# A relative-bias table stored with the head as its inner index, built first and loaded on the weights' queue

## The chip, the cores and the metric

The kernel runs on one core of a Trainium2 chip. The metric is the device time of one execution in microseconds (us), lower is better. Engines are named as in the profile: PE is TensorE's matmul, PEld its weight load, DVE VectorE, ACT ScalarE, POOL GpSimd, SP SyncE. DMAs are issued by two engines here: SP (queue q1, which carries the weights) and ACT (queue q10).

## What is computed

One decoder layer on 256 tokens of width 1024, in float32: softmax attention with 8 heads and a relative-position bias, then a mixture of 32 experts of which each token uses 4. Each sublayer is followed by a layer norm of the scaled residual sum. The attention, cut to what matters (there is one block of 256 keys, so every query sees all keys at or before it):

```python
qkv = (x @ w_in).reshape(B, S, 3, H, Dh)
s_own = einsum('bhqd,bhjd->bhqj', q, k) * Dh ** -0.5 + rel_t[:, t5_bucket(rel_own)]
s_own = where(rel_own >= 0, s_own, -inf)
o = einsum('bhqj,bhjd->bhqd', softmax(s_own), v)
return o @ w_out
```

Here `rel_own` is the distance from query to key, `t5_bucket` maps it to one of 32 buckets, and `rel_t` is the transpose of the learnt table `rel_bias` (32 buckets by 8 heads). The expert weights are nearly all of the 424 MB that are read.

## The kernel before

**Buffers.** SBUF holds 13 slots of 2 MB (`slot`, L102). Three are taken for good: `xhl`, `BT_xT` (the bias table BT in its first half, the transposed input xT in its second) and `QT_KTt`. The others hold weight tiles and their split copies `whl`. `todo` lists the weight tiles in the order of their use: six tiles of `w_in` in the order 0, 2, 1, 3, 4, 5, two of `w_out`, then for every expert four `w_gu` and two `w_dn`. `fetch` (L127) issues the next tile on SP, in pieces; `prefetch` (L140) does so whenever a slot is free. So the weights run ahead of the work by as many slots as are free, and no further.

**Order.** The order on each engine is the order of the program (`manual_schedule`). Each DMA takes one of eight completion semaphores in turn (DMAHW0 to DMAHW7, SP's and ACT's DMAs together), and a DMA waits until the one that had its semaphore before it has landed.

**The projections.** A loop over n = 0 to 11 (L394) takes half a tile of `w_in` per turn. A weight half tile is split into a high and a low part (`split`, L156: cast on ACT, L176; difference on DVE, L165), one turn ahead. In turns 0 to 7 `proj_qk` (L299) makes 48 matmuls of 256 columns per turn (L310 to L312), for Q and K; in turns 8 to 11 `proj_v` makes 24 of 512 columns. After two turns `evac` (L315) copies four PSUM banks out, on DVE and ACT. The banks of turns 4 and 5 are used again in turns 6 and 7.

**The attention between them.** After turn 4 `scores` (L348) makes the scores of head 0, after turn 5 of head 1, and so on. One turn later `softmax` (L354) scales them and adds the bias (`scalar_tensor_tensor` on DVE, L359, the only reader of BT), takes the maximum (L362) and the exponential (ACT, L364). Heads follow up to turn 11.

**The bias.** `rb` (32 by 8) and a one-hot `oh` (32 by 256) are loaded on SP behind the first weight tile (L248, L249). In turn 1 `rel_bias` (L261) multiplies them to 8 by 256 and copies that behind 127 columns of -1e30 into `rrow` (8 by 383, head as row). In turn 2 ACT stores it to DRAM as `rd`, in turn 3 ACT loads BT from it (L272): partition p, head h takes 256 numbers from column p on, so 1,024 runs of 1 KB with 1 MB in all. L359 reads BT backwards.

**The start.** Nine warm-up matmuls (L256) run on PE while xT and the first weight tile w0 arrive, w0 in six pieces (L245, then `load` at L247 for the last two).

The first lines of the softmax before, which the change touches:

```python
for t, (lo, hi) in enumerate(SPANS):
    nc.vector.scalar_tensor_tensor(p[:, lo:hi], ps[:, lo:hi], SC, BT[:, hh, :hi - lo][:, ::-1],
                                   op0=OP.mult, op1=OP.add)
```

Of the kernel before, what the change touches and what calls it, by code (L numbers as in the profile page):

```python
# [11 lines left out]
F32 = mybir.dt.float32  # L12
# [10 lines left out]
S, D, H, DH = 256, 1024, 8, 128  # L23
# [8 lines left out]
NEG = -1.0e30  # L32
# [28 lines left out]
def tile_decoder_layer(ctx: ExitStack, tc, a, out):  # L61
    nc = tc.nc
# [3 lines left out]
    dr = ctx.enter_context(tc.tile_pool(name="dr", bufs=1, space=DRAM))  # L66
    pm = ctx.enter_context(tc.tile_pool(name="pm", bufs=1, space=PSUM))

    def bank(name):
        return pm.tile([128, 512], F32, name=name)  # L70
# [11 lines left out]
    def small(name, w, p=128, dt=F32):  # L82
        return cst.tile([p, w], dt, name=name)

    c = small("c", C_W)
# [16 lines left out]
    def slot(name, dt=F32):  # L102
        used[0] += 1
        assert used[0] <= W_SLOTS
        return wp.tile([128, SLOT], dt, name=name, tag="w")
# [8 lines left out]
    def source(key):  # L114
        kind, e, k = key
        if kind == "in":
            return a["w_in"][e]
        return a["w_out"][k] if kind == "out" else a["w_gu" if kind == "gu" else "w_dn"][e, k]
# [8 lines left out]
    def fetch(pieces=1):  # L127
        key = todo.pop()
        src = source(key)
        t = slot("w").rearrange("p (k c) -> p k c", k=src.shape[1])  # L130
        load(t, src, pieces)
        w_tiles[key] = t

    def load(t, src, pieces):
        k = src.shape[1]
        for i in range(pieces):
            ks = slice(i * k // pieces, (i + 1) * k // pieces)
            nc.sync.dma_start(t[:, ks], src[:, ks])

    def prefetch():  # L140
        while todo and W_SLOTS - used[0] > reserve[0]:
            fetch(1 if len(todo) > 1 else 4)
# [74 lines left out]
    hp = hctx.enter_context(tc.tile_pool(name="hp", bufs=1))  # L217
# [5 lines left out]
    g7, sg = KTt[:, :512], KTt[:, 512:1024]  # L223
    aT = g7.rearrange("p (j s c) -> p j s c", j=4, s=2)
    Y = KTt[:, 1024:].rearrange("p (b c) -> p b c", b=2)
    BT, QT, KTt = (t.rearrange("p (h s) -> p h s", h=H) for t in (BT, QT, KTt))
    rb = hp.tile([32, H], F32, name="rb")
    oh_wg = hp.tile([128, 256], F32, name="oh_wg")
    oh, wg = oh_wg[:32], oh_wg.rearrange("p (k e) -> p k e", k=KT)
    rrow = hp.tile([H, 383], F32, name="rrow")  # L230
    zeros = hp.tile([128, 128], BF, name="zeros")
    zeros4 = zeros[:, None, :].to_broadcast([128, 4, 128])
    p3 = pp.tile([128, 3, 384], F32, name="p3", tag="p3")
    router = hp.tile([128, KT + 1, NE], F32, name="router")
    wr, br = router[:, :KT], router[:, KT]
    oh_, ol_ = xh, xl

    xT3 = xT.rearrange("p (k s) -> p k s", k=KT)
    key0 = todo.pop()
    w0 = w_tiles[key0] = slot("w").rearrange("p (k c) -> p k c", k=KT)  # L240
# [4 lines left out]
        nc.sync.dma_start(w0[:, i:i + 1], source(key0)[:, i:i + 1])  # L245
    nc.sync.dma_start(xT3[:, X_PARTS[2]], a["xT"][:, X_PARTS[2]])
    load(w0[:, 4:], source(key0)[:, 4:], 2)  # L247
    nc.sync.dma_start(rb, a["rel_bias"])  # L248
    nc.sync.dma_start(oh, a["onehot"])  # L249
    for _ in range(2):  # L250
        fetch(2)
    nc.vector.memset(ones, 1.0)
    nc.vector.memset(eps, EPS)
    warm = bank("tp2")
    for i in range(9):
        nc.tensor.matmul(warm[:, :128], ones, ones, start=i == 0, stop=i == 8)  # L256
    nc.vector.memset(rrow[:, 0:127], NEG)
    nc.vector.memset(zeros, 0.0)
    rd = dr.tile([H, 383], F32, name="rd")

    def rel_bias():  # L261
        pr = bank("tp2")
        nc.tensor.matmul(pr[:H, :256], rb, oh, start=True, stop=True)
        nc.vector.tensor_copy(rrow[:, 127:383], pr[:H, :256])
        nc.sync.dma_start(c, a["consts"])
        nc.sync.dma_start(router.rearrange("p k e -> p (k e)"), a["router"])

    def rel_bias_out():
        nc.scalar.dma_start(rd, rrow)

    def rel_bias_in():
        nc.scalar.dma_start(BT, bass.AP(tensor=rd.tensor, offset=rd.offset, ap=[[1, 128], [383, H], [1, S]]))  # L272

    def split_x(s):
        xhf, xlf = (t.rearrange("p k s -> p (k s)") for t in (xh, xl))
# [12 lines left out]
    def split_next(key):  # L288
        n = ahead.get(key)
        if n and n not in split_done:  # L290
            split_done.add(n)
            split(n, act_copy)
# [22 lines left out]
    def evac(blk, dst):  # L315
        ps = open_ps[blk]
        if blk < 4:
            h0 = (blk % 2) * 4
            for j in range(4):
                (nc.scalar.copy if j % 2 else nc.vector.tensor_copy)(dst[:, h0 + j, :], ps[j][:, :S])  # L320
        else:
            c0 = (blk % 2) * 512
            nc.scalar.copy(V[:, 0, c0:c0 + 512], ps[0])
            nc.vector.tensor_copy(V[:, 1, c0:c0 + 512], ps[1])
# [17 lines left out]
    SC = DH ** -0.5  # L342
# [5 lines left out]
    def scores(hh):  # L348
        ps = bank(next(rows_bank))
        nc.tensor.matmul(ps[:, 0:128], QT[:, hh, 0:128], KTt[:, hh, 0:128], start=True, stop=True)  # L350
        nc.tensor.matmul(ps[:, 128:384], QT[:, hh, 128:256], KTt[:, hh, :], start=True, stop=True)
        P[hh] = ps

    def softmax(hh):  # L354
        ps = P[hh]
        p = p3[:, hh % 3]
        st = hp.tile([128, 8], F32, name="sst", bufs=3)
        for t, (lo, hi) in enumerate(SPANS):
            nc.vector.scalar_tensor_tensor(p[:, lo:hi], ps[:, lo:hi], SC, BT[:, hh, :hi - lo][:, ::-1],  # L359
                                           op0=OP.mult, op1=OP.add)  # L360
        for t, (lo, hi) in enumerate(SPANS):
            nc.vector.tensor_reduce(st[:, t:t + 1], p[:, lo:hi], axis=AX.X, op=OP.max, negate=True)  # L362
        for t, (lo, hi) in enumerate(SPANS):
            nc.scalar.activation(p[:, lo:hi], p[:, lo:hi], AF.Exp, bias=st[:, t:t + 1],  # L364
                                 accum_out=st[:, 2 + t:3 + t])
        P[hh] = p, st

    def softmax_norm(hh):
        p, st = P[hh]
        nc.vector.reciprocal(st[:, 4:6], st[:, 2:4])  # L370
        for t, (lo, hi) in enumerate(SPANS):
            nc.vector.tensor_scalar(p[:, lo:hi], p[:, lo:hi], st[:, 4 + t:5 + t], None, op0=OP.mult)


    def p_transpose(hh):
        p, st = P.pop(hh)
        ps = bank(next(one_bank))
        for i in range(3):
            s = slice(i * 128, (i + 1) * 128)
            nc.tensor.transpose(ps[:, s], p[:, s], ident)  # L380
        nc.scalar.copy(QT[:, hh, :], ps[:, :256])
        nc.scalar.copy(KTt[:, hh, :128], ps[:, 256:384])
# [11 lines left out]
    for n in range(12):  # L394
        blk, i = ORDER[n // 2], n % 2
        last = n == 11
        if not last:
            split_next(("in", blk, i))
        if n == 1:
            rel_bias()  # L400
            reserve[0] = 1
            prefetch()
        if n == 2:
            rel_bias_out()
        if n == 3:
            rel_bias_in()
        for hh in score_at.get(n - 1, []):
            softmax(hh)
        if last:
            for hh in score_at.get(n - 1, []):  # L410
                softmax_norm(hh)
            split_next(("in", blk, i))
        (proj_qk if blk < 4 else proj_v)(blk, i)
        if i == 1:
            evac(blk, QT if blk < 2 else KTt)
        if not last:
            for hh in score_at.get(n - 1, []):
                softmax_norm(hh)
        for hh in score_at.get(n, []):
            scores(hh)  # L420
        for hh in trans_at.get(n, []):
            p_transpose(hh)
# [219 lines left out]
    h = x  # L642
# [219 lines left out]
    for p in range(NE // 2):  # L862
        ahead_pair = p + 1 < NE // 2
        for s in range(2):
            e = 2 * p + s
# [83 lines left out]
    lo, hi = HALVES  # L949
# [53 lines left out]
```

## Time and profile before

| | |
|---|---|
| median of 3 runs | 1087.15 us (1087.0 to 1087.31) |
| the profiled execution's own time | 1087.11 us |
| its span, first to last instruction | 1085.3 us |
| PE busy | 975.1 us (90% of the span) |
| DVE, ACT busy | 265.6 us (24%), 180.5 us (17%) |
| read from HBM | 423.91 MB, 392 GB/s over the span |
| first matmul of the projections / end of the last one | 5.42 us / 109.6 us |

What lies around the span is 1.8 us. The profile is one execution, taken by the hardware profiler. A busy PE there is not a PE at its peak, since matmuls overlap in the records. The idle time of an engine is put down to what ended it. The profile cuts the span in 40 slices of 27.1 us; one digit is the share of a slice in tenths.

### The profile page before, as it was taken

To read this page: it belongs to the slowest core of one execution; us is meant where nothing else is said; L and a number is where in the kernel's file an instruction comes from. 1 tells how busy PE (TensorE), PEld (TensorE's weight loads), DVE (VectorE), ACT (ScalarE), POOL (GpSimd) and SP (SyncE) were. 2 spreads that over 40 slices of the span, in tenths; PEclk is the share of its full clock that TensorE was granted. 3 is DMA by queue.
4 is the path that set the end of the run, shared out by engine and by line. 5 is a ranking of instruction groups with operands and counts; after the bars stand their busy time and mean duration, and the time that the engine had idled before them with its cause. 6 is when DMAs were issued, how large, how long until landed. Compare 5 with 4: busy or idle time off the path is not lost. (4 is left out here: it accounts for less than half of the span.)

```text
span 1085.3 us, 11473 instructions
## 1 busy us (share of the span) xinstructions
PE 975.1 (90%) x4886; PEld 450.4 (41%) x4886; DVE 265.6 (24%) x555; ACT 180.5 (17%) x345; POOL 15.7 (1%) x10
## 2 busy tenths in 40 slices
PE   9649989999999999888989889999989898988893
PEld 8648764334343443232424243343423243333331
DVE  5237562121222211112121232212111212121104
ACT  5126431101011110010101010011101010101112
POOL 0000030000000000000000000000000000000001
PEclk9869989999999999999999989999999999999997
DMA  9964579999999999999999999999999999999981
GB/s 358 422 243 152 161 297 406 428 427 428 428 426 428 428 425 430 427 427 429 426 429 428 413 423 426 428 428 427 427 428 427 428 429 428 428 428 426 429 372 40
DMA packets 33204, 425.74 MB, mean 392 GB/s; under 512 B 3672, under 2 KB 5120, under 8 KB 7456
## 3 DMA queue, kind: packets, MB, share of 16 engines
q1 hardware_dynamic: 31824, 422.87, 92.8%
q10 hardware_dynamic: 1328, 2.11, 0.6%
q8 instruction: 40, 0.66, 0.2%
q14 instruction: 12, 0.10, 0.0%
HBM read 423.91 MB, written 1.06 MB: 392 GB/s over the span
## 5 line engine op out<-in xcount | busy, mean ns | idle before, releaser
L677 PE MATMUL hg<-w,QT_KTt 128*64 128x512 f32 x960 | 250.8, 599 | 54.5 <-DMA w<-in_w_gu 54.2
L677 PE MATMUL hu<-w,QT_KTt 128*64 128x512 f32 x960 | 248.6, 594 | 0.0
L705 PE MATMUL yp<-w,QT_KTt 128*64 128x512 f32 x1008 | 226.8, 595 | 1.3 <-ACT QT_KTt L695 1.3
L684 DVE TENSOR_SCALAR QT_KTt<-hg 128x512 f32<-128x512 f32 x32 | 22.1, 692 | 665.5 <-PE hg L677 665.5
L677 PEld LDWEIGHTS hg<-w,QT_KTt 128*64 128x64 f32 x960 | 66.0, 137 | 194.9 <-issue 127.0
L705 PEld LDWEIGHTS yp<-w,QT_KTt 128*64 128x64 f32 x1008 | 70.6, 137 | 142.3 <-issue 127.9
L677 PEld LDWEIGHTS hu<-w,QT_KTt 128*64 128x64 f32 x960 | 71.2, 137 | 135.7 <-issue 135.7
L685 ACT ACTIVATE QT_KTt<-QT_KTt 128x512 f32<-128x512 f32 x32 | 20.1, 629 | 477.7 <-DVE QT_KTt L684 477.7
L709 ACT COPY QT_KTt<-yp 64x512 f32<-64x512 f32 x63 | 36.5, 580 | 233.4 <-PE yp L705 225.9
L663 PEld LDWEIGHTS tp<-OH,BT_xT 128*128 128x128 f32 x480 | 58.4, 199 | 12.0 <-issue 11.2
L663 PE MATMUL tp<-OH,BT_xT 128*128 128x128 f32 x480 | 62.7, 286 | 0.0
L165 DVE TENSOR_TENSOR whl<-w,whl 128x1024 fp32r<-128x1024 f32 (+1 forms) x36 | 41.2, 1187 | 29.4 <-ACT whl L176 29.4
L310 PE MATMUL o<-xhl,whl 128*128 128x256 f32 x48 | 15.0, 312 | 25.1 <-DVE QT_KTt L320 24.5
L176 ACT CAST whl<-w 128x1024 fp32r<-128x1024 f32 (+1 forms) x36 | 32.7, 954 | 11.3 <-DMA w<-in_w_in 4.7
L569 DVE TENSOR_SCALAR QT_KTt<-tp,c 128x128 f32<-128x128 f32 x60 | 20.5, 405 | 44.1 <-PE tp L663 44.1
L733 PE MATMUL tp<-QT_KTt 128*128 128x512 f32 x60 | 30.7, 593 | 0.0
L733 PE MATMUL o<-QT_KTt 128*128 128x512 f32 x60 | 29.8, 618 | 0.0
L571 ACT ACTIVATE QT_KTt<-tp,c 128x128 f32<-128x128 f32 x60 | 22.6, 457 | 36.3 <-PE tp L663 36.3
L695 ACT COPY QT_KTt<-tp 128x512 f32<-128x512 f32 x32 | 19.2, 600 | 42.9 <-PE tp L694 35.9
L686 DVE TENSOR_SCALAR hu<-hu 128x512 f32<-128x512 f32 x32 | 22.4, 700 | 3.1 <-PE hu L677 0.2
L694 PE MATMUL tp<-c,QT_KTt 128*128 128x128 f32 x128 | 20.0, 280 | 3.4 <-DVE QT_KTt L688 3.2
L688 DVE SCALAR_TENSOR_TENSOR QT_KTt<-hu,QT_KTt 128x512 f32<-128x512 f32 x32 | 22.1, 691 | 1.1
(258 smaller groups left out, 758.7 us busy)
## 6 DMA issues: line engine op xcount, KB each, us to landing
w<-in_w_gu SPq DMA_DIRECT2D x128, 2048.0 KB, 39.1
w<-in_w_dn SPq DMA_DIRECT2D x63, 2048.0 KB, 39.1
w<-in_w_in SPq DMA_DIRECT2D x3, 2048.0 KB, 21.1
w<-in_w_in SPq DMA_DIRECT2D x4, 1024.0 KB, 11.1
w<-in_w_out SPq DMA_DIRECT2D x2, 2048.0 KB, 28.3
w<-in_w_dn SPq DMA_DIRECT2D x4, 512.0 KB, 31.8
w<-in_w_in SPq DMA_DIRECT2D x4, 256.0 KB, 5.7
w<-in_w_in SPq DMA_DIRECT2D x2, 512.0 KB, 8.5
```

The lines of the kernel that those rows point to most:

```text
L165: nc.vector.tensor_tensor(lo[:, s], w[:, s], hi[:, s].bitcast(F32), op=OP.subtract)
L176: nc.scalar.copy(o, i)
L569: nc.vector.tensor_scalar(o, i, g, b, op0=OP.mult, op1=OP.add)
L571: nc.scalar.activation(o, i, AF.Identity, scale=g, bias=b)
L663: nc.tensor.matmul(ps[:, k * 128:(k + 1) * 128], h[:, t, kk * 128:(kk + 1) * 128], OH[:, t].rearrange("p s c -> p (s c)"), start=t == 0, s ...
L677: nc.tensor.matmul(hgu[i][s * 64:(s + 1) * 64], xg(k), w[:, kk, q * 512:(q + 1) * 512], start=False, stop=k == KT - 1)
L684: nc.vector.tensor_scalar(g7, hgu[0], LIMIT, None, op0=OP.min)
L686: nc.vector.tensor_scalar(u7, u7, LIMIT, -LIMIT, op0=OP.min, op1=OP.max)
L688: nc.vector.scalar_tensor_tensor(sg, u7, 1.0, g7, op0=OP.add, op1=OP.mult)
L705: nc.tensor.matmul(y_ps[s], aT[:, kk % 4, kk // 4, :], w[:, k, HALVES[s ^ swap]], start=kk == 0, stop=kk == KT - 1)
L709: copy(Y[s * 64:(s + 1) * 64, s ^ swap, :], y_ps[s])
L733: nc.tensor.matmul(po, GT[:, cb, t, :], Y[:, cb, :], start=True, stop=True)
```

## The change

`rel_bias` and `rel_bias_out`, `rel_bias_in` of turns 1 to 3 are gone. In their place, ahead of the loop: ACT issues the loads of `rb` and `oh` before anything else. PE multiplies them after the warm-up, with 128 distances as output rows and 8 heads as columns, twice. DVE copies the result into `rrow` (now 128 by 3 by 8). ACT stores it to `rd` (now 383 rows of 8 heads) in two DMAs: 127 rows of -1e30, and 256 rows of bias. SP then loads BT between the second and the third tile of `w_in`: partition p takes 2,048 consecutive numbers from row p on. L359 reads BT with a step of 8 numbers, backwards. The loads of `consts` and `router` stay in turn 1.

```diff
-    BT, QT, KTt = (t.rearrange("p (h s) -> p h s", h=H) for t in (BT, QT, KTt))
+    BT_rows, BT = BT, BT.rearrange("p (s h) -> p s h", h=H)
+    QT, KTt = (t.rearrange("p (h s) -> p h s", h=H) for t in (QT, KTt))
...
-    rrow = hp.tile([H, 383], F32, name="rrow")
+    rrow = hp.tile([128, 3, H], F32, name="rrow")
...
+    nc.scalar.dma_start(rb, a["rel_bias"])
+    nc.scalar.dma_start(oh, a["onehot"])
...
-    nc.sync.dma_start(rb, a["rel_bias"])
-    nc.sync.dma_start(oh, a["onehot"])
-    for _ in range(2):
-        fetch(2)
...
+    rd = dr.tile([383, H], F32, name="rd")
+
+    def rel_rows(row, ap):
+        return bass.AP(tensor=rd.tensor, offset=rd.offset + row * H, ap=ap)
+
+    pr = bank("yp")
+    for i in range(2):
+        nc.tensor.matmul(pr[:, i * H:(i + 1) * H], oh[:, i * 128:(i + 1) * 128], rb, start=True, stop=True)
+    nc.vector.tensor_copy(rrow[:, :2], pr[:, :2 * H].rearrange("p (i h) -> p i h", i=2))
+    nc.scalar.dma_start(rel_rows(0, [[H, 127], [1, H]]), rrow[:127, 2])
+    nc.scalar.dma_start(rel_rows(127, [[H, 128], [128 * H, 2], [1, H]]), rrow[:, :2])
+    fetch(2)
+    nc.sync.dma_start(BT_rows, rel_rows(0, [[H, 128], [1, S * H]]))
+    fetch(2)
...
-            nc.vector.scalar_tensor_tensor(p[:, lo:hi], ps[:, lo:hi], SC, BT[:, hh, :hi - lo][:, ::-1],
+            nc.vector.scalar_tensor_tensor(p[:, lo:hi], ps[:, lo:hi], SC, BT[:, :hi - lo, hh][:, ::-1],
```

How this moves the instructions is seen at two places. The first is the head of ACT's order, before (L numbers of the kernel before):

```order
L176 ACT_TABLE_LOAD
L176 CAST xhl<-BT_xT 128x256 [waits DMAHW0_49]
L176 CAST whl<-w 128x512 [waits DMAHW1_49]
L176 CAST xhl<-BT_xT 128x256 [waits DMAHW2_49]
L176 CAST whl<-w 128x512 [waits DMAHW3_49]
```

and with the change (L numbers of the changed kernel):

```order
L239 DMA rb<-in_rel_bias 32x8
L240 DMA oh_wg<-in_onehot 32x256
L267 DMA rd<-rrow 127x8 [waits DVE_49]
L268 DMA rd<-rrow 128x2x8 [waits DMAHW1_49,DVE_49]
L176 ACT_TABLE_LOAD
L176 CAST xhl<-BT_xT 128x256
L176 CAST whl<-w 128x512 [waits DMAHW3_49]
```

Four DMAs stand ahead of ACT's table load and its first casts; the fourth waits for DVE's copy into `rrow`. The second place is SP's queue from the third input part of xT on, before:

```order
L246 DMA BT_xT<-in_xT 128x1024
L138 DMA w<-in_w_in 128x1024
L138 DMA w<-in_w_in 128x1024 [waits DMAHW0_49]
L248 DMA rb<-in_rel_bias 32x8 [waits DMAHW1_49]
L249 DMA oh_wg<-in_onehot 32x256 [waits DMAHW2_49]
L138 DMA w<-in_w_in 128x2048 [waits DMAHW3_49]
L138 DMA w<-in_w_in 128x2048 [waits DMAHW4_49]
L138 DMA w<-in_w_in 128x2048 [waits DMAHW5_49]
L138 DMA w<-in_w_in 128x2048 [waits DMAHW6_49]
```

and with the change:

```order
L249 DMA BT_xT<-in_xT 128x1024 [waits DMAHW2_49]
L138 DMA w<-in_w_in 128x1024 [waits DMAHW3_49]
L138 DMA w<-in_w_in 128x1024 [waits DMAHW4_49]
L138 DMA w<-in_w_in 128x2048 [waits DMAHW5_49]
L138 DMA w<-in_w_in 128x2048 [waits DMAHW6_49]
L270 DMA BT_xT<-rd 128x2048 [waits DMAHW7_49,DMAHW1_49]
L138 DMA w<-in_w_in 128x2048 [waits DMAHW0_49]
L138 DMA w<-in_w_in 128x2048
```

`rb` and `oh` are gone from SP, BT stands among the tiles of `w_in`, and the semaphores that SP waits on are others. Of these, DMAHW4 was last used by the first store of `rd` (127 rows), DMAHW1 by the second: the sixth piece of w0 (the second row of 128x1024) waits until the first store has landed, and BT waits for the second.

## Rows read from the trace of the kernel before

**Rows 1.** The page's 40 slices: DMA share in tenths, rate.
```profile
DMA  9964579999999999999999999999999999999981
GB/s 358 422 243 152 161 297 406 428 427 428 428 426 428 428 425 430 427 427 429 426 429 428 413 423 426 428 428 427 427 428 427 428 429 428 428 428 426 429 372 40
```
**Rows 2.** Waits of PE, whole span: us in total, times, longest us.
```profile
PE hg L677 <- DMA w<-in_w_gu: 54.2, 48, 2.3
PE o L310 <- DVE QT_KTt L320: 24.5, 1, 24.5
```
**Rows 3.** Waits of DVE, 0 to 200 us.
```profile
DVE p L359 <- DMA BT_xT<-rd: 28.5, 1, 28.5
```
**Rows 4.** DMA issues: line's tile, engine, count, KB each, median us to landing.
```profile
BT_xT<-rd ACTq DMA_DIRECT2D x1, 1024.0 KB, 37.1
...
BT_xT<-in_xT SPq DMA_DIRECT2D x1, 128.0 KB, 2.6
```
**Rows 5.** Windows by stage: PE, PEld, DVE, ACT, POOL busy; PEclk, DMA share, GB/s.
```profile
50.00:60.00 10.00, 0.00 (x0) 0.00 (x0) 0.00 (x0) 0.00 (x0) 0.00 (x0) 0.50 1.01 421
60.00:70.00 10.00, 1.14 (x5) 1.17 (x6) 2.52 (x9) 1.91 (x7) 0.00 (x0) 0.50 0.49 200
...
80.00:90.00 10.00, 10.00 (x61) 8.88 (x60) 7.29 (x19) 4.94 (x14) 0.00 (x0) 1.00 0.14 34
...
160.00:170.00 10.00, 10.00 (x48) 3.30 (x46) 2.93 (x17) 2.84 (x4) 0.00 (x0) 1.00 0.67 247
170.00:180.00 10.00, 9.87 (x64) 5.78 (x62) 4.04 (x8) 2.61 (x6) 0.00 (x0) 1.00 1.01 434
```
**Rows 6.** Timeline of PE around its long wait: start us, us, instruction.
```profile
43.77 0.60 PE L351 MATMUL hu<-QT_KTt 128*128 128x256 f32 x2
68.86 0.55 PE L310 MATMUL o<-xhl,whl 128*128 128x256 f32 x1 [24.49 <-DVE QT_KTt L320]
...
71.56 0.37 PE L310 MATMUL o<-xhl,whl 128*128 128x256 f32 x1
...
72.00 0.28 PE L310 MATMUL o<-xhl,whl 128*128 128x256 f32 x1
72.12 0.28 PE L311 MATMUL o<-xhl,whl 128*128 128x256 f32 x1
```
**Rows 7.** Timeline of all engines at the start.
```profile
0.74 1.28 ACT L176 ACT_TABLE_LOAD   x1 [0.74 <-PEq L995]
...
1.06 4.21 PE L256 MATMUL tp<-ones 128*128 128x128 f32 x18 [1.06 <-DVE ones L252]
...
3.32 0.40 ACT L176 CAST xhl<-BT_xT 128x256 fp32r<-128x256 f32 x1 [1.30 <-DMA BT_xT<-in_xT]
...
4.75 0.62 ACT L176 CAST whl<-w 128x512 fp32r<-128x512 f32 x1 [1.02 <-DMA w<-in_w_in]
...
13.03 1.14 ACT L176 CAST whl<-w 128x512 fp32r<-128x512 f32 x2 [0.21 <-DMA w<-in_w_in]
...
13.49 0.59 PE L263 MATMUL tp<-oh_wg,rb 32*8 32x256 f32 x2
```
**Rows 8.** Timeline of ACT, 14 to 31 us.
```profile
20.06 0.37 ACT L320 COPY QT_KTt<-tp 128x256 f32<-128x256 f32 x1 [0.35 <-PE tp L312]
...
24.78 0.55 ACTq L269 DMA_DIRECT2D rd<-rrow  x1
...
30.00 0.39 ACTq L272 DMA_DIRECT2D BT_xT<-rd  x1
```
**Rows 9.** Groups of DVE by form, 60 to 130 us.
```profile
L362 DVE TENSOR_REDUCE sst<-p 128x1 f32<-128x256 f32 x8 | 3.3, 411 | 0.0
...
L359 DVE SCALAR_TENSOR_TENSOR p<-hu,BT_xT 128x256 f32<-128x256 f32 x4 | 1.7, 416 | 0.0
...
L489 DVE TENSOR_REDUCE BT_xT<-oh_wg 128x32 f32<-128x256 f32 x1 | 0.6, 625 | 0.0
```
**Rows 10.** Timeline of PE at the end of the projections.
```profile
110.61 0.70 PE L387 MATMUL tp<-QT_KTt,BT_xT 128*128 128x256 f32 x2 [0.30 <-ACT QT_KTt L382]
```

More of the change, by code (lines that the diff above doesn't have):

```diff
@@ L256, in tile_decoder_layer @@
         nc.tensor.matmul(warm[:, :128], ones, ones, start=i == 0, stop=i == 8)
-    nc.vector.memset(rrow[:, 0:127], NEG)
+    nc.vector.memset(rrow[:, 2], NEG)
     nc.vector.memset(zeros, 0.0)
[L259 to L272, printed above, removed]
+    rd = dr.tile([383, H], F32, name="rd")
[10 more added lines that the diff above has]
+    fetch(2)
     def split_x(s):
@@ L399, in tile_decoder_layer @@
         if n == 1:
-            rel_bias()
+            nc.sync.dma_start(c, a["consts"])
+            nc.sync.dma_start(router.rearrange("p k e -> p (k e)"), a["router"])
             reserve[0] = 1
             prefetch()
[L403 to L406, printed above, removed]
         for hh in score_at.get(n - 1, []):
```

## The prediction, made before the changed kernel was run

> **What bounds the kernel now.** I read the slices first [rows 1]. From about 165 us to the end the DMA rate stands at 428 GB/s with its engines 9 tenths busy or more. There the weights' stream sets the pace, and PE waits for it, 54.2 us in 48 pieces [rows 2]. The expert phase can't be shortened by anything in this change, but it can begin earlier. For the DMA is not full before it: the third to the sixth slice (54 to 163 us) run at 243, 152, 161 and 297 GB/s. There the missing rate is (185 + 276 + 267 + 131) / 428 x 27.1 us = 54 us of an idle stream. It idles because the 13 slots are full and the work that frees them is late. The stream becomes full for good at about 165 us [rows 5]. So the end is that moment plus fixed bytes: a microsecond gained in the work ahead of 165 us is a microsecond at the end, as long as no more than those 54 us are taken.
>
> What is late in that work? PE's second long wait is one of 24.5 us, for a DVE copy at L320 [rows 2]. DVE had itself waited 28.5 us for the load of BT [rows 3]. The timeline of PE has the place: scores of head 1 at 43.77 us, next projection matmul at 68.86 [rows 6]. The copies that free the PSUM banks of turns 4 and 5 stand behind `softmax(0)` on DVE, and that waits for BT. BT was issued at 30.0 us [rows 8] and took 37.1 us to land [rows 4], with DMA full until about 65 us [rows 5].
>
> Why 37.1 us for 1 MB: its 1,024 runs are 64 for each of 16 DMA engines, 0.58 us each. A weight row of 16 KB takes 16,384 B x 16 / 427 GB/s = 0.61 us. So a run of BT had about one weight row beside it each time.
>
> **The change, part by part.** The sum is made against the profiled execution: 1087.11 us, of which 1085.3 are span. The median of the three runs is 1087.15, so no correction is needed.
>
> *The wait goes: -24.5 us.* SP now issues BT behind the second tile of `w_in`. Its 128 rows of 8 KB stand in the line of the weights and cost 1 MB / 425 GB/s = 2.5 us. If both stores to `rd` have landed by 15 us, BT lands near 20 us. Turn 5's softmax wants it at about 39 us (67.2 us less the 28.5 waited [rows 3]). The work that comes then takes the place of the wait: after the scores at 43.77 us PE goes straight on, since the bank it needs has its last matmul about 1 us before the turn's end and the copy takes 0.4 us. What is late next is nothing on PE up to the end of the projections. The tile of turn 6 is the fourth; 10 MB in all, BT counted, have landed by 28 us at 425 GB/s.
>
> *The slow clock after it: -1.3 us.* During the wait the granted clock fell to 0.5 [rows 5]. Twelve matmuls then ran at half rate, 68.86 to 71.56 us [rows 6], 2.7 us where twelve take 1.44 at the pitch of 0.12 that follows. Without the wait there is no fall.
>
> *The start is later: +1.7 us.* This is the change's new cost. ACT issues four DMAs ahead of its table load, and the fourth waits for DVE's copy, that for two PE matmuls, and those stand behind the warm-up, which ends at 1.06 + 4.21 = 5.3 us [rows 7]. Loads of `rb` and `oh`, issued at about 0.8 and 1.2 us, land before that (2.6 us for a piece of xT [rows 4]). The two matmuls take at most the 0.59 us of the old one with 256 columns [rows 7], the copy and the semaphores some 0.3 (a copy of 256 columns takes 0.37 on ACT [rows 8]), the store's issue 0.4 to 0.55 [rows 8]. The table load of 1.28 us, off the path before [rows 7], begins near 6.6 and ends at 7.9. The first two casts (0.40 and 0.62 [rows 7]) follow, and PE's first projection matmul starts near 8.9 us instead of 5.4. Most of these 3.5 us are made good: before, turns 0 and 1 waited for pieces of w0 (the casts of the last one at 13.03 us waited for a DMA [rows 7]) and ended at 20.0 us (ACT's last copy waits for PE until 20.06 [rows 8]). Now PE has 96 matmuls of 0.12 us, 11.5 us, which end at 20.4; with twelve at half rate, as after the long wait, 21.7. Against 20.0 that is +1.7. The least is +0.4, with a clock that stays up; the most depends on the sixth piece of w0, below.
>
> *The strided read: +0.6 us.* L359 now steps 32 bytes in BT. No such read of L359 is in the trace; the nearest is L489, a reduction that steps through 256 elements, 625 ns against 411 for the unit-step one of L362 [rows 9]. That is 0.84 ns an element, 0.32 us for a head's 384, 2.6 us for eight on DVE. PE covers it in turns 5 to 10, where DVE is busy 7.29 of 10 us and PE all of it [rows 5]. At the end of the projections the cover is gone: PE waits 0.30 us there already [rows 10]. So I take the last two heads, 0.6 us; the bounds are 0 and 2.6. The Trainium skill ("SBUF — State Buffer", the note on cachelines under the DMA port swizzle) speaks against this layout: SBUF has 16-byte lines, each crossing to a new line pays a penalty, and 4 float32 is as far as one can step free. It gives no size; by it every element pays, and L489, at 625 ns, agrees that there is a price. If it were double what L489 shows, the sum would be 0.6 us higher.
>
> *Edits at nothing.* The old `rel_bias` work in turns 1 to 3 (a matmul of 0.59 us, two issues) goes from under other waits. The bytes of BT stay 1 MB. The stores are 12 KB.
>
> Sum: -24.5 - 1.3 + 1.7 + 0.6 = -23.5, so 1087.1 - 23.5 = **1063.6 us**.
>
> **The rivals.** *Slower: the first store holds the weights' queue.* SP's sixth piece of w0 waits for the 127-row store. If these rows, a number that 16 doesn't divide, all go through one DMA engine and each is served like a run of BT, they take 127 x 0.58 = 74 us and land at 75. The piece lands 2.6 us after its issue, is cast in 0.6, and leaves PE two slices of 1.44; so turn 1 ends 6.1 us after the store. Landing at 15.6 us costs nothing beyond the 21.7 above, each microsecond later costs one, and break-even is at 39 us. At 75 the time is 1063.6 + 59 = 1123 us. The Trainium skill ("DMA: Bandwidth & Descriptors", on why a DMA increments its semaphore by 16) says that a DMA from ACT uses the largest count up to 16 that divides the outer sizes, so 127 partitions use one engine. No row here shows it. For the rival: the old store was never timed on landing. Against: the 0.58 us are a weight row's own time, and while SP waits, only 8 DMAs with 8 rows per engine stand ahead, done by 10 us; what is left of the 127 then runs alone.
>
> *A part given back:* the store lands between 20 and 39 us; 1068 to 1087.
>
> *Bytes decide:* the stream is the bound throughout and nothing comes earlier; 1087 us. Against it stand the 54 idle us.
>
> *The change doesn't do what it says:* BT is still late or another wait takes over in turns 5 to 6; half the gain, 1075 us. For it: BT waits for the second store, which stands behind the first. Against: some 20 us of slack.
>
> **Chances.** The forecast 0.83, a part given back 0.06, slower 0.04, bytes 0.03, BT still late 0.04. The range: the bounds of the forecast are -25.8 + 0.4 = 1061.7 and, with 2.6 for the read and the store at 20 us (+4.4), 1070.0; I take 1061.0 to 1069.5, which leaves out the other cases and little more. A measurement tells 0.2% (2.2 us) from no change. Faster by more than that: 0.83 + 0.06 + 0.04 = 0.93; within it 0.03; slower 0.04.
>
> **What would show it.** In the changed kernel's profile: no wait of DVE L358 for BT, PE without a gap at 44 to 69 us and no clock of 0.5 there; first projection matmul near 8.9 us, turn 1 ending near 21.7; L358 near 630 ns for 256 columns; DMA full for good near 142 us; PE's waits for `w_gu` still near 54 us. Wrong: a first store that lands after 16 us, a DMA gap in the first 30 us that PE feels, or a new wait of PE before 110 us.

## The result and the profile after

| | before | after |
|---|---|---|
| median | 1087.23 us (4 runs, 1087.0 to 1089.35) | **1064.06 us** (4 runs, 1063.89 to 1064.37) |
| the profiled execution: time, span | 1087.11, 1085.3 us | 1064.1, 1062.2 us |
| ratio | | 0.9782, 95% interval 0.9769 to 0.9795 |

The forecast was 1063.6 us, in a range of 1061.0 to 1069.5. L numbers below are those of the kernel named: in the changed one the projections are L309 to L311, their copies L319, the softmax's first step L358.

The waits of PE over the whole span (us in total, times, longest us) are the first view:

```profile
PE hg L673 <- DMA w<-in_w_gu: 55.8, 50, 2.2
...
PE o L309 <- ACT whl L176: 3.0, 1, 3.0
```

The 24.5 us of [rows 2] are gone. The waits for the weights are 55.8 us against 54.2: the expert phase is what it was, only earlier. New is one wait of 3.0 us, at the start. The timeline of DVE where the 28.5 us wait for BT stood [rows 3] (start us, us, instruction, idle time before it):

```profile
43.80 0.93 DVE L358 SCALAR_TENSOR_TENSOR p<-hg,BT_xT 128x128 f32<-128x128 f32 x2
44.65 0.61 DVE L361 TENSOR_REDUCE sst<-p 128x1 f32<-128x128 f32 x2
45.77 0.42 DVE L319 COPY QT_KTt<-o 128x256 f32<-128x256 f32 x1 [0.51 <-PE o L311]
```

No idle time stands ahead of L358, and the copy that frees a bank for turn 6 follows at 45.77 us. It waits for PE, not PE for it. The windows (PE, PEld, DVE, ACT, POOL busy; PEclk, DMA share, GB/s):

```profile
50.00:60.00 10.00, 10.00 (x84) 9.90 (x84) 6.89 (x16) 4.23 (x12) 0.00 (x0) 1.00 1.02 428
60.00:70.00 10.00, 10.00 (x52) 8.42 (x51) 5.70 (x14) 6.04 (x16) 0.00 (x0) 1.00 1.01 428
140.00:145.00 5.00, 5.00 (x26) 1.69 (x24) 1.46 (x6) 0.82 (x1) 0.00 (x0) 1.00 0.89 301
145.00:150.00 5.00, 5.00 (x25) 1.52 (x21) 0.69 (x1) 0.03 (x1) 0.00 (x0) 1.00 1.01 433
```

PE is busy throughout 50 to 70 us at the full clock, where [rows 5] had 1.14 us of work at 0.50. The DMA engines are full for good from 140 to 145 us on, not from 160 to 170. The page's slices show the same: the stretch without full DMA has become shorter by about one slice.

```profile
DMA  9986689999999999999999999999999999999981
GB/s 355 426 344 221 251 362 428 429 428 427 428 426 429 427 429 426 427 428 428 429 428 426 415 426 429 427 429 426 428 428 426 429 426 428 426 430 426 430 364 41
```

The DMA issues (KB, us to landing) and the waits of SP's queue from 0 to 40 us tell how BT came in time. The first store of `rd` held the queue for 0.7 us, BT waited 7.3 us for the second one, was issued at 15.3 us and landed 6.1 us later, at 21.4, where turn 5 wants it at 43.8. So it had 22 us to spare.

```profile
BT_xT<-rd SPq DMA_DIRECT2D x1, 1024.0 KB, 6.1
...
rd<-rrow ACTq DMA_DIRECT2D x1, 8.0 KB, 9.6
```

```profile
SPq L270 <- DMA rd<-rrow: 7.3, 1, 7.3
...
SPq L138 <- DMA rd<-rrow: 0.7, 1, 0.7
```

The start is where something was lost. Its timeline:

```profile
4.58 2.72 SPq L138 DMA_DIRECT2D w<-in_w_in  x4
4.87 0.52 PEld L265 LDWEIGHTS yp<-rb,oh_wg 32*128 32x128 f32 x4
4.87 0.61 PE L265 MATMUL yp<-rb,oh_wg 32*128 32x8 f32 x4
5.51 0.17 DVE L266 COPY rrow<-yp 128x16 f32<-128x16 f32 x1 [4.41 <-PE yp L265]
5.72 0.43 ACTq L268 DMA_DIRECT2D rd<-rrow  x1
6.18 1.28 ACT L176 ACT_TABLE_LOAD   x1 [6.18 <-DVE rrow L266]
...
8.45 0.58 PE L309 MATMUL o<-xhl,whl 128*128 128x256 f32 x1 [2.97 <-ACT whl L176]
```

The chain is as forecast: matmul, copy, store, table load, cast. The first projection matmul starts at 8.45 us, before it was 5.42. But the windows of the same stretch show a clock of 0.50 (1.2 GHz) for longer than the working allowed:

```profile
7.00:8.00 1.00, 0.00 (x0) 0.00 (x0) 0.09 (x1) 0.99 (x3) 0.00 (x0) 0.93 1.11 397
8.00:9.00 1.00, 0.55 (x2) 0.50 (x2) 0.91 (x2) 1.00 (x3) 0.00 (x0) 0.50 0.98 363
...
13.00:14.00 1.00, 1.00 (x6) 1.00 (x6) 1.00 (x3) 0.95 (x2) 0.00 (x0) 0.50 0.98 410
14.00:15.00 1.00, 1.00 (x8) 1.00 (x7) 1.00 (x3) 0.00 (x0) 0.00 (x0) 0.66 1.06 443
15.00:16.00 1.00, 1.00 (x10) 1.00 (x9) 0.41 (x1) 0.51 (x1) 0.00 (x0) 1.00 1.04 442
```

PE idled from 5.48 to 8.45 us; the clock fell in that time and came back between 14 and 15 us. 27 matmuls, from 8.45 to 14.67 us, ran at half rate. Turn 1 ended with this copy on ACT, 3.1 us later than the 20.06 of [rows 8]:

```profile
23.16 0.37 ACT L319 COPY QT_KTt<-tp 128x256 f32<-128x256 f32 x1 [0.35 <-PE tp L311]
```

What stands under the projections' end, at last:

```profile
87.71 0.70 PE L386 MATMUL tp<-QT_KTt,BT_xT 128*128 128x256 f32 x2 [0.30 <-ACT QT_KTt L381]
```

This row answers to [rows 10]. It comes 110.61 - 87.71 = 22.9 us earlier, and the span is 23.1 us shorter: what was gained ahead of it arrived at the end.

### The profile page after: what moved, and what is told of

Same layout as the page of the kernel before. It is cut to its first block, busy times and chain, and to the rows that moved or that the text cites. A ratio compares the mean times of both kernels' runs of the same rounds, so it can differ in the third digit from the quotient of the medians.

```text
span 1062.2 us, 11476 instructions
## 1 busy us (share of the span) xinstructions
PE 973.1 (92%) x4888; PEld 449.7 (42%) x4888; DVE 267.6 (25%) x555; ACT 179.9 (17%) x345; POOL 15.7 (1%) x10
## 5 line engine op out<-in xcount | busy, mean ns | idle before, releaser
L673 PE MATMUL hg<-w,QT_KTt 128*64 128x512 f32 x960 | 250.9, 599 | 55.9 <-DMA w<-in_w_gu 55.8
L659 PE MATMUL tp<-OH,BT_xT 128*128 128x128 f32 x480 | 61.7, 283 | 0.0
L165 DVE TENSOR_TENSOR whl<-w,whl 128x1024 fp32r<-128x1024 f32 (+1 forms) x36 | 41.2, 1187 | 24.9 <-ACT whl L176 24.8
L683 DVE TENSOR_TENSOR QT_KTt<-QT_KTt 128x512 f32<-128x512 f32 x32 | 21.9, 684 | 0.0
## 6 DMA issues: line engine op xcount, KB each, us to landing
w<-in_w_in SPq DMA_DIRECT2D x3, 2048.0 KB, 20.3
```

What stands on the lines that cost most here:

```text
L165: nc.vector.tensor_tensor(lo[:, s], w[:, s], hi[:, s].bitcast(F32), op=OP.subtract)
L659: nc.tensor.matmul(ps[:, k * 128:(k + 1) * 128], h[:, t, kk * 128:(kk + 1) * 128], OH[:, t].rearrange("p s c -> p (s c)"), start=t == 0, s ...
L673: nc.tensor.matmul(hgu[i][s * 64:(s + 1) * 64], xg(k), w[:, kk, q * 512:(q + 1) * 512], start=False, stop=k == KT - 1)
L683: nc.vector.tensor_tensor(g7, g7, sg, op=OP.mult)
```

## The experiments

Three things changed at once: how BT lies (8 KB rows, read by L358 with a step), when it is made (ahead of all, not in turns 1 to 3), and on which queue it is loaded. Theory A, that of the prediction: only the time of landing counts, against 44 us. The rivals: it is the large rows, or the queue. Early alone, layout alone and queue alone were each run; layout and queue together but late were not. The start was a question of its own. All the ratios are to runs of the kernel before on the same chip, whose medians were 1088.04 and 1088.43 us there. One row is followed through all of the experiments: the first matmul of the p-transposes after the projections, 110.61 us before and 87.71 after.

**Early, but in the old layout** (two kernels, against the changed one). BT goes back to 1,024 runs of 1 KB and L358 to unit step; ACT issues the load behind its first casts in the one, SP behind the second tile of `w_in` in the other.

```diff
-    rd = dr.tile([383, H], F32, name="rd")
+    rd = dr.tile([H, 383], F32, name="rd")
...
-        nc.tensor.matmul(pr[:, i * H:(i + 1) * H], oh[:, i * 128:(i + 1) * 128], rb, start=True, stop=True)
+    nc.tensor.matmul(pr[:H, :256], rb, oh, start=True, stop=True)
...
+    nc.scalar.dma_start(rd, rrow)
+    def rel_bias_in(engine):
+        engine.dma_start(BT, bass.AP(tensor=rd.tensor, offset=rd.offset, ap=[[1, 128], [383, H], [1, S]]))
...
+    rel_bias_in(nc.scalar)
```

The other has `rel_bias_in(nc.sync)` between the two fetches.

On ACT's queue:

> Early alone: the table is made as early as in the changed kernel, but with the head as outer index (1,024 runs of 1 KB, unit-step reads), and ACT issues its load at about 14 us, on its own queue. Theory A (each run is served beside one weight row, so 64 runs an engine set the landing): 16 runs beside 8 KB rows of 0.3 us, some beside the short rows of the constants, the rest beside 16 KB rows of 0.61 us: 26 to 34 us from issue to landing, so at 40 to 48 us, at or just behind turn 5's demand at 43.8; PE waits 0 to 6 us, total 1063.5 to 1069 us. Theory B (the load was late only because it was issued late, the layout is of no account): it lands about 6 to 10 us after its issue, no wait, 1064.0 us or less.

On SP's queue:

> Early and on the weights' queue, but with the head as outer index: 1,024 runs of 1 KB between the second and the third tile, unit-step reads. Theory A (in the line of the weights a run has nothing beside it, so the queue matters and not the run): landing within 4 to 8 us of the issue, L358's two forms back at 284 and 416 ns, total 1064.0 within 0.7 us, with the same late start. Theory B (short runs are slow by themselves): landing 20 us or more after the issue with the weight tiles behind it late; the tile of turn 4 would come after 25 us and PE would wait, 1066 us or more. If the strided read costs what I took for it (0.6 us), this kernel is that much faster than the changed one; if PE hides all of it, the same.

Measured: 1064.42 us (1064.12 to 1065.05), ratio 0.9782 [0.9765, 0.9798], and 1064.35 us (1064.02 to 1064.96), ratio 0.9781 [0.9765, 0.9798]. Both agree with the changed kernel's 0.9782. The DMA issue and the softmax of the one on ACT's queue:

```profile
BT_xT<-rd ACTq DMA_DIRECT2D x1, 1024.0 KB, 30.6
```

```profile
43.50 0.62 DVE L355 SCALAR_TENSOR_TENSOR p<-hg,BT_xT 128x128 f32<-128x128 f32 x2
```

Issued at 12.77 us, BT landed at 43.4, as long after its issue as Theory A had it (26 to 34 us), and was read at 43.50, with no wait. It was just in time, and any later landing would have been a wait. SP's weight loads stood 14.7 us in this kernel for the landing of BT, since a semaphore is taken in turn; that cost nothing in the total. The issue of the one on SP's queue:

```profile
BT_xT<-rd SPq DMA_DIRECT2D x1, 1024.0 KB, 9.0
```

There the same runs took 9.0 us, a little over the 4 to 8 that I expected, and BT landed at 20.3. So neither the 8 KB rows nor the queue is needed for this time; the queue gives 23 us of slack. That L355 takes 0.62 us for the two against 0.93 above shows the step's price on DVE, which PE hides.

**Layout and queue, each alone and late** (three kernels, against the kernel before). The first has BT's new layout in the old turns and on ACT's queue. The second is the same with 128 rows in the first store, not 127. The third is the kernel before with BT's load on SP's queue.

```diff
-    rd = dr.tile([H, 383], F32, name="rd")
+    rd = dr.tile([383, H], F32, name="rd")
...
-        nc.scalar.dma_start(rd, rrow)
+        nc.scalar.dma_start(rel_rows(0, [[H, 127], [1, H]]), rrow[:127, 2])
+        nc.scalar.dma_start(rel_rows(127, [[H, 128], [128 * H, 2], [1, H]]), rrow[:, :2])
...
-        nc.scalar.dma_start(BT, bass.AP(tensor=rd.tensor, offset=rd.offset, ap=[[1, 128], [383, H], [1, S]]))
+        nc.scalar.dma_start(BT_rows, rel_rows(0, [[H, 128], [1, S * H]]))
```

L365 then reads BT with the step of 8. With 127 rows:

> Layout alone: the kernel before with the head as inner index (BT in 128 rows of 8 KB), all work left in turns 1 to 3 and the load on ACT's queue. Theory A (what counts is how many pieces an engine has to serve beside 16 KB weight rows, 0.61 us each; the 127-row store is spread over the engines): the two stores, issued at about 25 us, need up to 24 x 0.61 = 15 us and land by 36 to 40 us, ACT waits for them, BT lands 6 us later at 42 to 46, PE waits 3 to 9 us in all; total 1064 to 1072 us. Rival (the 127 rows all go through one engine): 127 x 0.61 = 77 us, the store lands near 102 us, BT near 108, ACT stands still until then; total 1115 to 1135 us, slower than the kernel before.

Measured: 1092.87 us (1090.94 to 1093.26), ratio 1.0042 [1.0028, 1.0056]: 0.4% **slower than before**, and neither theory's number. Its DMA issues, and the waits of ACT and PE:

```profile
BT_xT<-rd ACTq DMA_DIRECT2D x1, 1024.0 KB, 4.6
...
rd<-rrow ACTq DMA_DIRECT2D x1, 8.0 KB, 38.1
```

```profile
ACT QT_KTt L326 <- DMA rd<-rrow: 36.0, 1, 36.0
```

```profile
PE o L316 <- ACT whl L176: 28.6, 2, 26.9
```

BT's large rows land in 4.6 us here, where the runs took 37.1 [rows 4], but the two are not alike: BT is issued at 62.9 us, with the DMA engines busy for 0.62 of the time; beside a full stream the same rows took 11.3 us (next kernel). BT must wait for the stores, which were issued at 24.2 and 24.8 us, into the full weights' stream, and the second landed after 38.1 us. That wait stands on ACT, at the issue of BT, and behind it the casts of `w_in`, so PE stood still too. The wait has moved from the load to the store.

The trace has every packet on ACT's queue, and these tell why neither number came. The rows of each DMA are followed by packets of 4 bytes: 16 for BT, 8 for the 8-row store of the kernel before, 16 for the second store here, and 1 for the store of 127 rows. The counts fit one from each engine that carried it. Fifteen of the second store's 16 had come by 38.9 us. From 39.4 to 60.9 us the remaining rows of 32 bytes went singly, 0.613 us apart (four times two together): one engine, and for each small row the time of a 16 KB weight row, as the rival had it. From 61.5 us on the weights that had been asked for were nearly all there (DMA share 0.36 up to 62.5), and the last 82 rows went within 0.5 us. So the rival had the path and the price right, and its 77 us were cut short because the stream ended.

With 128 rows (against the one with 127):

```diff
-    rd = dr.tile([383, H], F32, name="rd")
+    rd = dr.tile([384, H], F32, name="rd")
...
-        nc.scalar.dma_start(rel_rows(0, [[H, 127], [1, H]]), rrow[:127, 2])
-        nc.scalar.dma_start(rel_rows(127, [[H, 128], [128 * H, 2], [1, H]]), rrow[:, :2])
+        nc.scalar.dma_start(rel_rows(0, [[H, 128], [1, H]]), rrow[:, 2])
+        nc.scalar.dma_start(rel_rows(128, [[H, 128], [128 * H, 2], [1, H]]), rrow[:, :2])
...
-        nc.scalar.dma_start(BT_rows, rel_rows(0, [[H, 128], [1, S * H]]))
+        nc.scalar.dma_start(BT_rows, rel_rows(1, [[H, 128], [1, S * H]]))
```

> The same with 128 rows of -1e30 in the first store instead of 127, and everything after them one row later: 128 can be divided over 16 engines, 127 can't. Both theories give 1064 to 1072 us here. Where it equals the kernel with 127 rows, the odd number is of no account; where it is tens of us faster, the 127 rows went through one engine.

Measured: 1075.57 us (1075.09 to 1078.31), ratio 0.9889 [0.987, 0.9907]: 1.1% faster than before but outside the expectation. Its DMA issues, and the waits of ACT and PE:

```profile
BT_xT<-rd ACTq DMA_DIRECT2D x1, 1024.0 KB, 11.3
...
rd<-rrow ACTq DMA_DIRECT2D x1, 4.0 KB, 10.6
rd<-rrow ACTq DMA_DIRECT2D x1, 8.0 KB, 19.6
```

```profile
ACT QT_KTt L326 <- DMA rd<-rrow: 17.6, 1, 17.6
```

```profile
PE o L316 <- ACT whl L176: 8.9, 1, 8.9
```

One row more in the first store brought the second's landing from 38.1 to 19.6 us, and the time down by 17.3 us. ACT stood 17.6 us, and PE 8.9. The 384 small rows went from 27.8 to 43.3 us, on all 16 engines; that is 0.65 us for each of an engine's 24, near the 0.61 that I had put. What I had left out are the 3.5 us between the first issue and the first row, and BT took 11.3 us, not 6. The Trainium skill ("DMA: Bandwidth & Descriptors", on why a DMA increments its semaphore by 16) says that 127 partitions go to one engine and 128 to 16. The packets agree: 1 closing packet for the first store with 127 rows, 16 with 128.

BT on SP's queue alone (against the kernel before):

```diff
     def rel_bias_in():
-        nc.scalar.dma_start(BT, bass.AP(tensor=rd.tensor, offset=rd.offset, ap=[[1, 128], [383, H], [1, S]]))
+        nc.sync.dma_start(BT, bass.AP(tensor=rd.tensor, offset=rd.offset, ap=[[1, 128], [383, H], [1, S]]))
```

> Queue alone: the kernel before with BT's load issued by SP instead of ACT, in turn 3, all else as before. Theory A (in the line of the weights BT waits for the bytes ahead of it and for nothing else): about 22.4 MB are issued ahead, so it lands near 56 us instead of 67.2, and PE's wait falls from 24.5 to about 13 us; total 1075 to 1078 us. Rival (1 KB runs need the time by themselves, in any queue): lands at 67 us or later, 1087 us.

Measured: 1083.8 us (1082.14 to 1084.88), ratio 0.9955 [0.9939, 0.9972]: 0.5% faster, outside both expectations.

```profile
BT_xT<-rd SPq DMA_DIRECT2D x1, 1024.0 KB, 32.3
```

```profile
PE o L310 <- DVE QT_KTt L320: 19.4, 1, 19.4
```

SP issued it at 29.4 us, in turn 3 as before. So the weights' queue alone makes BT land at 61.7 us, not 67.1, and PE's wait falls from 24.5 to 19.4 us. That is some 5 us of the 23, where I had expected more than twice as much. BT's first run starts at 56.4 us, when the bytes ahead were through, as Theory A had it; but its 1,024 runs then take 4.6 us, which I had left out.

**The start: keep PE busy** (against the changed kernel). Eight more warm-up matmuls behind the bias.

```diff
+    for i in range(8):
+        nc.tensor.matmul(warm[:, :128], ones, ones, start=i == 0, stop=i == 7)
```

> The changed kernel with eight more warm-up matmuls behind the two of the bias, so that PE is busy from 5.5 us to the first projection matmul. Theory A (the start costs 3.1 us because the clock falls at 7.9 us and 27 matmuls run at half rate, 2.5 us of it): the granted clock stays up, turn 1 ends at 20.3 to 20.9 us instead of 23.1, total 1061.3 to 1062.2 us. Theory B (the late ACT chain sets the start, the clock is beside the point): turn 1 ends at 23 us, 1064 us.

Measured: 1062.46 us (1062.24 to 1063.47), ratio 0.9765 [0.9749, 0.9781]. The windows of the start and the copy that ends turn 1:

```profile
5.00:8.00 3.00, 2.95 (x22) 2.55 (x20) 0.17 (x1) 1.31 (x2) 0.00 (x0) 1.00 1.03 384
8.00:14.00 6.00, 4.83 (x38) 4.63 (x39) 5.50 (x9) 6.00 (x12) 0.00 (x0) 1.00 1.02 393
```

```profile
21.24 0.37 ACT L321 COPY QT_KTt<-tp 128x256 f32<-128x256 f32 x1 [0.35 <-PE tp L313]
```

PE is now idle for 0.99 us ahead of its first projection matmul, not 2.97; the clock stays at 1.00 (2.4 GHz), and turn 1 ends 1.9 us earlier. The intervals of this kernel's ratio and the changed one's overlap (0.9749 to 0.9781, 0.9769 to 0.9795); the gain rests on the traces, where the followed row comes at 85.79 us instead of 87.71, and on the four runs, which all lie below the eight of the two early kernels with the old layout on the same chip (1062.24 to 1063.47 against 1064.02 to 1065.05). Turn 1 ends a little later than the 20.3 to 20.9 us that I expected: the second store was issued at 6.22 us instead of 5.72, the table load stands behind it, and the first matmul comes at 8.95 us instead of 8.45. From that matmul to the end of turn 1 it is 12.29 us here and 14.71 in the changed kernel. So some 2.4 of the 3.1 us that the start lost were the clock.

**The start: the store behind the casts** (against the changed kernel). DVE's copy comes behind the third cast of xT, the second store behind the fourth, and BT behind the third tile of `w_in`.

```diff
-    nc.vector.tensor_copy(rrow[:, :2], pr[:, :2 * H].rearrange("p (i h) -> p i h", i=2))
+    def rel_bias_copy():
+        nc.vector.tensor_copy(rrow[:, :2], pr[:, :2 * H].rearrange("p (i h) -> p i h", i=2))
+
+    def rel_bias_out():
+        nc.scalar.dma_start(rel_rows(127, [[H, 128], [128 * H, 2], [1, H]]), rrow[:, :2])
+        nc.sync.dma_start(BT_rows, rel_rows(0, [[H, 128], [1, S * H]]))
...
+    rel_bias_copy()
     split_x(slice(1024, 2048))
+    rel_bias_out()
```

> The changed kernel with the copy and the second store moved behind the casts of xT, so that ACT waits for nothing at its start, and BT's load behind the third tile. Theory A (the only cost of the change is ACT's wait at the start): first projection matmul at 5.4 to 5.8 us, turn 1 ends at 20.0 to 20.6, BT lands at 22 to 30 us with no wait of DVE for it, total 1061.0 to 1061.9 us. Rival (BT or the third tile comes late, since the store is later): DVE waits for BT at 43 us or ACT for the third tile at 25; 1064 us or more.

Measured: **1059.44 us** (1058.29 to 1060.31), ratio 0.9737 [0.9721, 0.9753]; it beats the kernel before and the changed one, and by more than expected. ACT's timeline at the start:

```profile
2.23 1.28 ACT L176 ACT_TABLE_LOAD   x1 [2.23 <-issue]
...
4.80 0.62 ACT L176 CAST whl<-w 128x512 fp32r<-128x512 f32 x1 [0.88 <-DMA w<-in_w_in]
...
6.62 0.62 ACT L176 CAST whl<-w 128x512 fp32r<-128x512 f32 x1 [0.33 <-DMA w<-in_w_in]
...
9.89 0.40 ACTq L271 DMA_DIRECT2D rd<-rrow  x1
...
18.19 0.37 ACT L326 COPY QT_KTt<-tp 128x256 f32<-128x256 f32 x1 [0.29 <-PE tp L318]
```

The first cast of a weight is at 4.80 us, near the 4.75 of [rows 7], and turn 1 ends at 18.19 us: 5.0 us before the changed kernel, and 1.9 before the kernel before. The first projection matmul comes at 5.93 us, a little later than expected. The store is issued at 9.89 us and lands 10.1 us later, BT is issued at 20.06 and lands 5.9 later, at 26.0; the first softmax reads it at 38.83, so 13 us are to spare. The part of 1.9 us I had not expected. The second piece of w0 is cast at 6.62 us here and at 7.74 before; the bias's matmul of 0.59 us is out of turn 1 as well. Why the piece lands sooner was not tried.

**Both together, with the old layout** (against the last one): the bias head-outer again, one store of 8 rows, 1 KB runs, on SP's queue.

```diff
+    rd = dr.tile([H, 383], F32, name="rd")
...
+    def rel_bias_out():
+        nc.scalar.dma_start(rd, rrow)
+        nc.sync.dma_start(BT, bass.AP(tensor=rd.tensor, offset=rd.offset, ap=[[1, 128], [383, H], [1, S]]))
```

> The kernel with the later stores (1059.4 us), but with the head as outer index: one store of 8 rows, 1,024 runs of 1 KB on the weights' queue behind the third tile, unit-step reads. Theory A (the layout is of no account once the load stands in the weights' line in time): the store lands within 4 us, BT about 9 us after its issue, total 1059.4 within 1 us. Rival (the rows are what makes it fast): 1061 us or more.

Measured: 1059.79 us (1058.95 to 1062.73), ratio 0.9734 [0.9717, 0.975]: the same. BT took 11.1 us, 2 more than expected, and nothing waited for it. Once the load is early and on the weights' queue, the layout is worth nothing that can be measured.

The row that was followed, in the profiled execution of each, against the kernel before. Turn 1 ends with the copy on ACT that was shown above for some of them; "from end to begin" is the time from there to the row:

| kernel | turn 1 ends, us | p-transposes begin, us | from end to begin, us | begin against before | span, us | span against before |
|---|---|---|---|---|---|---|
| before | 20.06 | 110.61 | 90.55 |  | 1085.3 |  |
| layout alone, 127 rows | 20.11 | 114.08 | 93.97 | +3.5 | 1089.2 | +3.9 |
| layout alone, 128 rows | 19.58 | 98.32 | 78.74 | -12.3 | 1073.5 | -11.8 |
| queue alone | 19.62 | 106.04 | 86.42 | -4.6 | 1081.8 | -3.5 |
| after | 23.16 | 87.71 | 64.55 | -22.9 | 1062.2 | -23.1 |
| early, runs, ACT's queue | 22.66 | 87.20 | 64.54 | -23.4 | 1062.4 | -22.9 |
| early, runs, SP's queue | 22.58 | 87.13 | 64.55 | -23.5 | 1062.3 | -23.0 |
| after, PE kept busy | 21.24 | 85.79 | 64.55 | -24.8 | 1060.5 | -24.8 |
| after, store behind the casts | 18.19 | 82.74 | 64.55 | -27.9 | 1056.5 | -28.8 |
| the same, old layout | 18.06 | 82.61 | 64.55 | -28.0 | 1060.6 | -24.7 |

In all but the last kernel the end follows this row one for one, within 1.1 us. The last one's profiled execution is the slowest of its four (1062.73 us); there 3.3 us were lost behind the row, and why was not settled.

The time from end to begin takes the start out of the comparison. In all six kernels that load BT early it is 64.5 to 64.6 us, with the old layout as with the new one and on either queue. In the kernel before it is 90.55. So everything that BT's lateness cost there is 26.0 us, the wait and the slow clock behind it, and all that sets the early kernels apart in this row was made by the end of turn 1.

## Why the prediction held, step by step

*The end follows the work ahead of the stream.* Right; the table above has it for both signs, with one execution as an exception. The stream became full at 140 to 145 us, as forecast.

*The wait goes: -24.5.* Right, and so is the reason: the load's landing. The experiments add which part of the change does it: the earliness, which alone brings all of the gain. Late, the large rows changed the time by +4.4 us with 127 rows in the first store and by -12.9 with 128, and the queue by -4.6.

*The slow clock after it: -1.3.* As forecast: 1.00 from 50 to 70 us. Wait and clock together were put at 25.8 us, and the table has 26.0.

*The start: +1.7 forecast, +3.1 measured.* This is the term that was mis-sized. The first matmul came at 8.45 us, 0.45 earlier than worked out; the clock was what I had wrong. I took twelve matmuls at half rate from the one case that the trace had [rows 6]. There were 27, and they took 6.22 us where 27 x 0.12 = 3.2 are full rate, a loss of 3.0 against the 1.3 allowed. So 21.7 - 0.45 + 1.7 = 22.95 us, where PE goes over to turn 2; the copy follows at 23.16. With the clock kept up, 2.4 us came back. Twelve was a count from another gap, and nothing said that it holds for this one.

*The strided read: +0.6 forecast, 0 measured.* The group of L358 on DVE, 30 to 110 us:

```profile
L358 DVE SCALAR_TENSOR_TENSOR p<-hu,BT_xT 128x256 f32<-128x256 f32 x4 | 2.6, 638 | 0.0
```

638 ns against 416 [rows 9] is the price that L489 foretold (about 630), so the rule of the Trainium skill ("SBUF — State Buffer", the note on cachelines under the DMA port swizzle) on a step beyond a cacheline agrees with this trace too. But PE hid all of it: the wait ahead of the p-transposes is 0.30 us, as before [rows 10], and with unit-step reads the table's time from turn 1's end to the p-transposes is the same. The cover that I thought gone at the end held.

The sum with the measured terms is -24.5 - 1.3 + 3.1 = -22.7 us, and the profiled executions differ by 23.0. The two errors, +1.4 and -0.6, partly cancelled each other; that the total was nearer than its parts (0.5 us off) is luck.

*The rivals.* The store of 127 rows did go through one engine, as the first rival had it: in the changed kernel too one closing packet follows it. But it did not hold the queue. SP waited 0.7 us for it and issued the sixth piece of w0 at 5.70 us, so it had landed by then, where 0.58 us for each row would have meant 75 us. Its rows went from 3.37 to 5.06 us, eight of them 0.12 us after the one before, nearly all others 0.006. So the argument against that rival, that most of the rows run alone so early, was the right one. The price that it named is real elsewhere: in the middle of the stream, in the kernel with the layout alone, a row of that store cost 0.613 us, the two stores took 38 us, and the kernel was slower than before. The other rivals fall with the result: the wait for BT is gone, and the end came 23 us earlier.

## What to carry to other kernels

Ask of a late load first when it has to land, and then issue it, and all that it waits for, early enough: here being early was worth the whole 23 us, while late the layout by itself changed the time by +4.4 or -12.9 us, after the rows of its store, and the queue by -4.6. A small store that has to travel beside a full weight stream can cost more than the megabyte that follows it, so it goes ahead of the stream or gets its time, and never stands on an engine whose next work others need. Count the rows of such a store too: 127 went through one engine, 128 through 16. Do not put a wait before an engine's first work: the pause at the start cost 3 us, most of it in the matrix engine's clock, and moving the store behind the first casts gave it back and more.

## What was not expected of the hardware

- After PE's 3 us of idle time from 5.48 us on, the granted clock was at 0.50 until 14 to 15 us, through 6 us of unbroken matmuls, 27 of them; after the 24.5 us wait of the kernel before it came back after 12.
- 127 rows of 32 bytes went through one engine and 128 through 16: the second store's landing beside the weight stream went from 38.1 to 19.6 us, and the time from 1092.87 to 1075.57 us.
- On one engine a row of 32 bytes took 0.613 us, the time of a 16 KB weight row, while the weights streamed on the other queue, and 0.006 us at the start of the changed kernel.
- The 1 MB of BT in 8 KB rows on ACT's queue beside the stream took 11.3 us, of which 3.5 passed before the first row; on SP's, in line with the weights, 5.9 to 7.1.
